# Moving z, the attention matrix and the transposes of q and v inside a hybrid layer's mixer

## The chip, the cores and the metric

The kernel runs on one core of a Trainium2 chip. The metric is the device time of one execution in microseconds, as the median of three runs. The engines are TensorE (PE, with its weight loads as PEld), VectorE (DVE), ScalarE (ACT), GpSimd (POOL) and SyncE (SP, which issues most DMAs). Each engine works through its own queue of instructions in order; an instruction that waits holds back all that stand behind it on that engine.

## The reference

One layer over 512 positions of width 1024. A mixer with two head groups (a gated delta rule and a sliding-window attention) is followed by a mixture of 32 experts, of which each token uses two.

```python
h = modulate(rms_norm(x, norm_mix[l]), shift1, scale1)
proj = h @ w_in[l]
(g_q, g_k, g_v, g_z, g_a, g_b, s_q, s_k, s_v) = jnp.split(proj, split_points, axis=-1)
gdn_out = gated_deltanet(g_q, g_k, g_v, g_z, g_a, g_b, conv_w[l], a_log[l],
                         dt_bias[l], gdn_out_norm[l])
swa_out = sliding_window_attention(s_q, s_k, s_v, q_norm[l], k_norm[l], sinks[l], positions)
mixed = jnp.concatenate([gdn_out, swa_out], axis=-1) @ w_out[l]
x = x + gate1[:, None, :] * mixed
h2 = modulate(rms_norm(x, norm_ffn[l]), shift2, scale2)
x = x + gate2[:, None, :] * hierarchical_moe(h2, ...)
```

In gated_deltanet q, k and v pass a short convolution with silu; per chunk of 64 positions a unit lower triangular matrix is inverted, `attn = (q k^T) * decay` is formed, and the chunks are scanned with a state. The result is normed and multiplied by silu(z). The sliding-window attention norms q and k, turns them by the angles of their positions (rope), and adds a sink per head to the softmax.

## The kernel before

Every product of the mixer is made in three passes: both operands are split into a high and a low part, and high x high, high x low and low x high are summed (`passes`, lines L263 to L265). A weight is split by ScalarE (high part, L269) and GpSimd (low part, L270) one step ahead of the projection that uses it (`split_w`, called from `project`). A projection of one block of 128 columns of q, k, v or z is 24 products of 128x512 into one bank (p_proj); one of 256 columns of the attention's q, k and v is 96 products of 128x256 (p_nat).

The program writes the mixer as five streams: `delta_rule` (convolution of k, decay, inversion, joins, chunks, gated output), `products` (all projections, the angles, rope's turns and the attention), `ropes`, `modulations` and `out_gdn` (gate rows, output weights, output projection of the delta rule's half). Each stream yields keys, and `weave` always runs the stream with the lowest key next; so the numbers after `yield` set the order in which the instructions are written, and that order is the order of each engine's queue, apart from small shifts by the scheduler.

The names that the change touches:

- `q_block` (L599), `v_block` (L621): after a projection's products the convolution on VectorE (L397, L400), then `to_rows`, four transposes on TensorE (p_q, p_v, L406). Before, these stand in the middle of the next projection's products.
- `attn(n)` (L605): for 128 positions, p_qk on TensorE (L611), the product with the decay on VectorE (an, L614), transposes on TensorE (p_at, L617), a copy on ScalarE (L618). Before, all four run while the blocks are inverted.
- the inversion: 31 steps of two VectorE instructions (prod L643, R L645), then eight transposes on VectorE (tw L657, Mn L662) with copies on ScalarE (TT L659). `join32` (p_y, p_z) and `join64` (p_yy) assemble the blocks on TensorE, and `chunk` scans them.
- `gate_z` (L783): evacuation and silu of one block of z.
- `angles` (L796): p_pos, a transpose of the positions on TensorE, then VectorE (L805 to L815), then a long row of 128x128 instructions on GpSimd (L816 to L834).
- `rope`, `rope_turn`, `attend`: scores p_s, softmax, transposes p_pT, p_av. `gdn_out(n)`: p_ot (L771) and the gated output.
- `gate_rows` (p_gate on TensorE, L986, copy kg on ScalarE, L989), `load_wo` (the output weights scaled by kg on VectorE, L1002, then split: woH on ScalarE, woL on GpSimd for the first four blocks), `router_operands` (p_cst, L1036). `out_half(1, tb, cc)` is 12 products of p_wo for 128 positions and 512 columns and an addition to xr (L1019); eight of these make the delta rule's half, and eight the attention's half follow. Then come routing, the gather of the tokens, and the experts.

Of the kernel before, what the change touches and what calls it, by code (L numbers as in the profile page):

```python
# [13 lines left out]
AF = mybir.ActivationFunctionType  # L14
ALU = mybir.AluOpType
# [4 lines left out]
P = 128  # L20
# [49 lines left out]
def hybrid_layer(ctx, tc, x, c, positions, w_ada, b_ada, norm_mix, w_in, conv_w, a_log, dt_bias,  # L70
# [187 lines left out]
    hH = [hHL[0][kb // 4][:, kb % 4] for kb in range(KB)]  # L258
    hL = [hHL[1][kb // 4][:, kb % 4] for kb in range(KB)]

    def passes(ps, aH, aL, bH, bL, first, last):

        T.matmul(ps, aH, bH, start=first, stop=False)  # L263
        T.matmul(ps, aH, bL, start=False, stop=False)  # L264
        T.matmul(ps, aL, bH, start=False, stop=last)  # L265

    def split(hi, lo, src, eng):

# [130 lines left out]
        A.activation(raw, y, AF.Tanh)  # L399
        V.scalar_tensor_tensor(y, raw, 1.0, y, op0=ALU.add, op1=ALU.mult)  # L400

    def to_rows(src, name):

        pt = pst([P, NT, P], name)
        for tb in range(NT):
            T.transpose(pt[:, tb], src[:, tb * P:(tb + 1) * P], ident)  # L406
        return pt

    def heads(t):
        return t.rearrange("p t (h d) -> p t h d", d=HD)  # L410
# [146 lines left out]
    def split_w(c0, h):  # L557
# [9 lines left out]
            slots.done(f"w{base}")  # L567
        pieces[c0, h] = t

    def project(c0, each, ahead=0):  # L570

        nat = c0 >= C_S
        ps = [psa([P, 2, 256], f"p_nat{c0}_{i}") for i in range(2)] if nat else psa([P, S], f"p_proj{c0 // P}")
        for h in range(2 if nat else 1):
            i = steps.index((c0, h))
            if i + 1 < len(steps):
                split_w(*steps[i + 1])
            w = pieces[c0, h]
            if nat:
                for tb in range(NT):  # L580
                    t = slice(tb * P, (tb + 1) * P)
                    for i in range(4):
                        kb = 4 * h + i

                        passes(ps[tb // 2][:, tb % 2], hH[kb][:, t], hL[kb][:, t], w[:, 0, i], w[:, 1, i],
                               kb == 0 and tb % 2 == 0, kb == KB - 1 and tb % 2 == 1)
            else:
                for kb in range(KB):
                    passes(ps, w[:, 0, kb], w[:, 1, kb], hH[kb], hL[kb], kb == 0, kb == KB - 1)
            slots.done(f"wH{c0}{h}")  # L590
        if nat:
            for tb in range(NT):
                each(tb, ps[tb // 2][:, tb % 2])
        else:
            each(c0 // P, ps)
        load_w(ahead)


    def q_block(cb, ps):  # L599
        qT = big["qT"]  # L600
        raw = big["qraw"][:, cb]
        conv_block(ps, cb, raw, qT[:, cb])
        head_sums(to_rows(qT[:, cb], f"p_q{cb}"), ssq[:, :, 2 * cb:2 * cb + 2], raw)

    def attn(n):  # L605

# [14 lines left out]
    def v_block(cb, ps):  # L621
        b = cb - 8
        t = fill_tile(f"cv{cb}")
        conv_block(ps, cb, big["vraw"][:, b], t)
        v_ = big["vb"][:, :, b * P:(b + 1) * P]
        A.activation(v_, to_rows(t, f"p_v{cb}"), AF.Copy)
        G.tensor_tensor(out=heads(v_), in0=heads(v_), in1=bc2(beta[:, :, 2 * b:2 * b + 2]), op=ALU.mult)


    def invert_prepare():  # L630
# [408 lines left out]


    mod = {}
    GDN_OUT = 112.

    def delta_rule():
        yield 0
# [39 lines left out]
                    hold_slot(f"TT{j}", [P, 16, P])  # L1085
                    G.memset(big[f"TT{j}"], 0.0)
        for cb in range(4):
            yield 66
            invert_finish(cb)
        slots.done("R")  # L1090
        join32(0)
        join64(0)
        join32(1)
        for n in range(NT):
            yield 67
            chunk(n)
            if n + 1 < NT:
                join64(n + 1)
            if n + 2 < NT:
                join32(n + 2)  # L1100
        yield 85
        slots.done("qT", "knat", "knT", "E0", "E1", "TT0", "TT1")
        yield GDN_OUT
        mix_tiles(1)
        for n in range(NT):
            yield GDN_OUT + .1 + 9. * n
            gdn_out(n)
        slots.done("vb", "gz")

    def products():  # L1110
        yield 9
        hold_slot("qT", [P, 4, S])
        hold_slot("qraw", [P, 4, S])
        split_w(*steps[0])
        for i in range(4):
            project(order[i], q_block, 1 - i % 2)
            yield 9 + 5 * i
        slots.done("qraw")
        hold_slot("vb", [P, NT, 512])
        hold_slot("vraw", [P, 4, S])  # L1120
        for i in range(4):
            project(order[4 + i], v_block, i % 2)
            yield 30 + 5 * i
# [5 lines left out]
        slots.done("vraw")  # L1129
        hold_slot("sr", [P, 2, D])  # L1130
        big["skv"] = big["sr"][:, 0].rearrange("p (t n) -> p t n", t=NT)
        project(C_S + 512, keep(big["skv"], 0), 1)
        hold_slot("sq_n", [P, NT, 512])
        yield 57
        project(C_S, keep(big["sq_n"], 0), 1)
        yield 67
        project(C_S + 256, keep(big["sq_n"], 256))
        angles()
# [12 lines left out]
        V.tensor_scalar(nsink, sink, -1.0, None, op0=ALU.mult)  # L1151
        hold_slot("kg", [P, 2, D])
        big["krT"], big["g1"] = big["kg"][:, 0].rearrange("p (k t) -> p k t", t=S), big["kg"][:, 1]
        hold_slot("qrT", [P, 4, S])
        mix_tiles(0)
        for tb in range(NT):
            yield 92.5
            rope_turn(tb)
        for tb in range(NT):
            yield 99. + 12. * tb  # L1160
            attend(tb, 0)
            yield 99. + 12. * tb + 12. / 2
            attend(tb, 1)
        slots.done("qrT", "sq_n", "sr")

    def ropes():
        yield 87.9
        big["ssh"], big["rsh"] = sm("ssh", (P, NT, NR)), sm("rsh", (P, NT, NR))
        for tb in range(NT):
            head_scale(tb)  # L1170
        rsqrt_n(big["rsh"], big["ssh"], 1.0 / HD)
        for tb in range(NT):
            yield 92.2 + 0. * tb
            rope(tb)

    def modulations():
# [14 lines left out]
                columns_e(ada_raw[2], 2, "A2e", 0, 1, col_e[:, 2])  # L1191

    def out_gdn():
        yield 96.
        router_operands()
        gate_rows(big["g1"], mod["g1"])
        xr[0] = pair.tile([P, NT, D], F32, tag="pair", name="xr")
        for i in range(2):
            nc.sync.dma_start(xr[0][:, 2 * i:2 * i + 2], x_view[:, 2 * i:2 * i + 2])
        yield 140.  # L1200
        load_wo(0)
        load_wo(1)
        for tb in range(NT):
            yield max(GDN_OUT + .15 + 9. * tb + 20., 140.)
# [686 lines left out]
```

## Time and profile before

| what | value |
|---|---|
| median of 3 runs | 691.93 us (690.79 to 701.05) |
| the profiled execution | 690.03 us, span 688.0 us |
| mean granted TensorE clock | 0.963 |
| busy in the span: TensorE, VectorE, ScalarE, GpSimd | 90%, 56%, 35%, 26% |
| the chain that ended last | TensorE 45%, DMA 27%, VectorE 20% |

The span is what the profiler saw of the program; the time of the execution has 2.0 us around it. Busy shares are means over stages with different limits, so the rows below are taken by stage.

### The profile page before, as it was taken

What the parts mean: (1) busy time and instruction counts of PE and PEld (TensorE: products, weight loads), DVE (VectorE), ACT (ScalarE), POOL (GpSimd) and SP (SyncE); (2) the same over time, 40 slices, a digit from 0 to 9 for tenths busy, and PEclk for the clock granted to TensorE, in tenths of its full rate; (3) what the DMA queues carried; (4) which work ended last, traced back from release to release, by engine and by line L of the source; (5) the groups of instructions that cost most, each with busy time, mean ns of one, the idle gap of its engine ahead of it and who ended that gap; (6) DMA issues with size and microseconds to landing.
All of it is one profiled execution on the core that took longest, in us unless ns stands there. A gap on an engine that the chain in (4) does not pass through costs nothing.

```text
span 688.0 us, 10766 instructions
## 1 busy us (share of the span) xinstructions
PE 621.2 (90%) x3907; PEld 378.7 (55%) x3908; DVE 387.2 (56%) x808; ACT 243.7 (35%) x546; POOL 182.2 (26%) x259
## 2 busy tenths in 40 slices
PE   6899799988888999988879998899999999999984
PEld 2576554646567978875447887334343334444521
DVE  3343986698999325688887348311342434444724
ACT  3235554232334442328772243413213232222200
POOL 2501315162263386063452002101001121111100
PEclk9799999997999999999989999999999999999998
DMA  8992374174310300251028849599999999999973
GB/s 256 293 318 65 122 279 164 62 250 162 123 61 23 102 2 12 90 216 62 1 64 302 335 156 354 203 399 416 412 414 403 411 410 406 408 408 410 408 296 123
DMA packets 62805, 161.78 MB, mean 235 GB/s; under 512 B 7175, under 2 KB 32931, under 8 KB 56608
## 3 DMA queue, kind: packets, MB, share of 16 engines
q1 hardware_dynamic: 57216, 148.52, 58.3%
q0 software_dynamic: 3952, 6.81, 2.9%
q10 hardware_dynamic: 1584, 5.77, 2.1%
q8 instruction: 31, 0.51, 0.3%
q14 instruction: 22, 0.18, 0.1%
HBM read 158.72 MB, written 8.39 MB: 243 GB/s over the span
## 4 chain that ended last, share of the span: by engine, by line
PE 45%; DMA 27%; DVE 20%; POOL 3%; issue 2%; ACT 2%; SPq 1%; POOLq 0%; ACTq 0%; DVEq 0%
DMA w_p<-in_w_up_dram 15%; DMA w_p<-in_w_down_dram 6%; PE p_gu L1600 5%; PE p_y L1636 3%; DMA w_p<-in_w_gate_dram 3%; DVE prod L643 3%; PE p_proj L265 3%; PE p_proj L263 3%; PE p_proj L264 3%; PE p_wo L264 2%; PE p_wo L265 2%; PE p_wo L263 2%; DVE cv L397 2%; DVE R L645 2%; PE p_ada L284 1%
## 5 line engine op out<-in xcount | busy, mean ns | idle before, releaser
L1600 PE MATMUL p_gu<-w_p,xT 128*32 128x512 f32 (+2 forms) x560 | 95.9, 594 | 0.0
L270 POOL TENSOR_TENSOR wH<-w,wH 128x512 fp32r<-128x512 f32 x36 | 52.4, 1472 | 125.9 <-ACT wH L269 112.8
L1600 PEld LDWEIGHTS p_gu<-w_p,xT 128*32 128x32 f32 (+2 forms) x560 | 32.0, 123 | 61.4 <-issue 55.8
L1519 POOL DMA_INDIRECT gb<-xn_d,ids x16 | 16.2, 1014 | 160.4 <-PE p_x L1587 146.4
L1636 PE MATMUL p_y<-w_p,hT 128*32 128x512 f32 (+2 forms) x280 | 51.3, 597 | 3.7 <-DVE hT L1624 2.6
L1609 DVE TENSOR_TENSOR hid<-hid,p_gu 128x256 f32<-128x256 f32 x16 | 6.7, 421 | 82.6 <-ACT hid L1608 82.6
L1608 ACT ACTIVATE hid<-p_gu 128x256 f32<-128x256 f32 x16 | 6.1, 384 | 126.8 <-PE p_gu L1600 126.8
L1593 ACT ACTIVATE xT<-p_x,sh2e,A2e 128x128 f32<-128x128 f32 x128 | 46.3, 467 | 12.1 <-PE p_x L1587 11.3
L1638 DVE SCALAR_TENSOR_TENSOR y<-p_y,wts,rsl 128x512 f32<-128x512 f32 x32 | 24.0, 749 | 41.5 <-PE p_y L1636 41.5
L265 PE MATMUL p_proj<-hH,wH 128*128 128x512 f32 x96 | 40.8, 425 | 0.0
L263 PE MATMUL p_proj<-hH,wH 128*128 128x512 f32 x96 | 40.5, 422 | 0.0
L264 PE MATMUL p_proj<-hL,wH 128*128 128x512 f32 x96 | 40.0, 417 | 0.0
L1656 PE MATMUL p_add<-yHL,to 128*128 128x512 f32 x128 | 35.5, 417 | 2.9 <-DVE xr L1661 1.9
L1656 PEld LDWEIGHTS p_add<-yHL,to 128*128 128x128 f32 x128 | 21.5, 188 | 19.7 <-DVE xr L1661 8.0
L1636 PEld LDWEIGHTS p_y<-w_p,hT 128*32 128x32 f32 (+2 forms) x280 | 14.8, 122 | 31.0 <-issue 24.4
L1661 DVE TENSOR_TENSOR xr<-xr,p_add 128x512 f32<-128x512 f32 x40 | 26.8, 686 | 6.9 <-PE p_add L1656 6.9
L263 PE MATMUL p_nat<-wH,hH 128*128 128x256 f32 x96 | 28.0, 291 | 0.0
L643 DVE TENSOR_TENSOR prod<-R 128x1 f32<-128x1 f32 (+30 forms) x31 | 27.2, 877 | 0.7
L265 PE MATMUL p_nat<-wH,hL 128*128 128x256 f32 x96 | 27.5, 286 | 0.0
L264 PE MATMUL p_nat<-wH,hH 128*128 128x256 f32 x96 | 27.5, 286 | 0.0
L263 PE MATMUL p_wo<-woH,mH 128*128 128x512 f32 x64 | 25.9, 404 | 0.0
L264 PE MATMUL p_wo<-woL,mH 128*128 128x512 f32 x64 | 25.7, 402 | 0.0
(523 smaller groups left out, 1362.2 us busy)
## 6 DMA issues: line engine op xcount, KB each, us to landing
w_p<-in_w_gate_dram SPq DMA_DIRECT2D x52, 512.0 KB
w_p<-in_w_up_dram SPq DMA_DIRECT2D x52, 512.0 KB
w_p<-in_w_down_dram SPq DMA_DIRECT2D x26, 1024.0 KB
ada<-in_w_ada_dram SPq DMA_DIRECT2D x16, 1024.0 KB
w<-in_w_in_dram SPq DMA_DIRECT2D x9, 1024.0 KB
ada<-in_w_ada_dram SPq DMA_DIRECT2D x12, 512.0 KB
w<-in_w_gate_dram SPq DMA_DIRECT2D x12, 512.0 KB
w<-in_w_up_dram SPq DMA_DIRECT2D x12, 512.0 KB
```

The costliest lines, as they stand in the source:

```text
L263: T.matmul(ps, aH, bH, start=first, stop=False)
L264: T.matmul(ps, aH, bL, start=False, stop=False)
L265: T.matmul(ps, aL, bH, start=False, stop=last)
L270: eng.tensor_tensor(out=lo, in0=src, in1=hi.bitcast(F32), op=ALU.subtract)
L643: V.tensor_tensor(out=pp, in0=Ti[:, :i, :i].rearrange("p j k -> p k j"), in1=Ms[:, :i, i][:, None, :].to_broadcast([P, i, i]), op=ALU.mult)
L1519: nc.gpsimd.indirect_dma_start(out=buf, out_offset=None, in_=xn_d[:, :], in_offset=bass.IndirectOffsetOnAxis(ap=ap, axis=0), bounds_check= ...
L1593: A.activation(self.xT[:, kb], pt[:, i], AF.Identity, bias=sh2e[:, kb:kb + 1], scale=A2e[:, kb:kb + 1])
L1600: self.last = T.matmul(self.ph[r], self.xT[:, kb, r], w[1 + kb // 4][:, :, kb % 4], start=(kb == 0), stop=(kb == KB - 1), tile_position=(0 ...
L1636: self.last = T.matmul(py[o:o + n], self.hT[:, i, o:o + n], w[3][:, i, cs], start=(i == 0), stop=(i == 1), tile_position=(0, o))
L1638: self.made = V.scalar_tensor_tensor(y[:, cs], py, self.w_ap, g2[:, cs], op0=ALU.mult, op1=ALU.mult).ins.name
L1656: t = T.matmul(ps, g_.to[:, tb * P:(tb + 1) * P], g_.yHL[:, i, cs], start=(2 * j + i == 0), stop=(2 * j + i == n - 1))
L1661: return V.tensor_tensor(out=x1(tb)[:, cs], in0=x1(tb)[:, cs], in1=ps, op=ALU.add).ins.name
```

## The change

Products of a projection are remembered by `last_mm`, and the transposes p_q and p_v are ordered behind the last product of the next projection (`rest`, `later`). `attn` moves from the inversion to the places between join and chunk. The keys of the streams change: z is written ahead of the joins, rope and attention are interleaved with the chunks and the gated output (GDN_STEP, ATT), and the gate rows and the output weights come behind the mixer.

```diff
     def passes(ps, aH, aL, bH, bL, first, last):
...
-        T.matmul(ps, aL, bH, start=False, stop=last)
+        last_mm[0] = T.matmul(ps, aL, bH, start=False, stop=last).ins.name
...
-    def to_rows(src, name):
+    def to_rows(src, name, after=None):
 
         pt = pst([P, NT, P], name)
         for tb in range(NT):
-            T.transpose(pt[:, tb], src[:, tb * P:(tb + 1) * P], ident)
+            t = T.transpose(pt[:, tb], src[:, tb * P:(tb + 1) * P], ident)
+            if after:
+                later(t, after)
         return pt
...
             slots.done(f"wH{c0}{h}")
+        while rest:
+            rest.pop(0)(last_mm[0])
         if nat:
...
-        head_sums(to_rows(qT[:, cb], f"p_q{cb}"), ssq[:, :, 2 * cb:2 * cb + 2], raw)
+        rest.append(lambda after: head_sums(to_rows(qT[:, cb], f"p_q{cb}", after), ssq[:, :, 2 * cb:2 * cb + 2], raw))
...
         conv_block(ps, cb, big["vraw"][:, b], t)
-        v_ = big["vb"][:, :, b * P:(b + 1) * P]
-        A.activation(v_, to_rows(t, f"p_v{cb}"), AF.Copy)
-        G.tensor_tensor(out=heads(v_), in0=heads(v_), in1=bc2(beta[:, :, 2 * b:2 * b + 2]), op=ALU.mult)
+
+        def rows_(after):
+            v_ = big["vb"][:, :, b * P:(b + 1) * P]
+            A.activation(v_, to_rows(t, f"p_v{cb}", after), AF.Copy)
+            G.tensor_tensor(out=heads(v_), in0=heads(v_), in1=bc2(beta[:, :, 2 * b:2 * b + 2]), op=ALU.mult)
+        rest.append(rows_)
...
-    GDN_OUT = 112.
+    GDN_OUT, GDN_STEP, ATT = 85., 2.2, 2.2
...
         join32(0)
         join64(0)
+        attn(0)
         join32(1)
         for n in range(NT):
-            yield 67
+            yield 72. + 4 * n
             chunk(n)
             if n + 1 < NT:
+                attn(n + 1)
                 join64(n + 1)
...
-                for n in range(NT):
-                    attn(n)
...
-        yield 78
         project(C_Z, gate_z, 1)
-        yield 82
+        yield 64
         project(C_Z + P, gate_z)
-        yield 88
+        yield 67
         project(C_Z + 2 * P, gate_z)
-        yield 92
+        yield 70
         project(C_Z + 3 * P, gate_z)
...
         for tb in range(NT):
-            yield 99. + 12. * tb
+            yield 75.3 + ATT * 2 * tb
             attend(tb, 0)
...
     def out_gdn():
-        yield 96.
+        yield 92.5
         router_operands()
         gate_rows(big["g1"], mod["g1"])
...
-        yield 140.
+        yield 92.6
         load_wo(0)
         load_wo(1)
```

In the queues this looks as follows (the changed kernel's lines have numbers that are 2 to 12 higher). On GpSimd before, around the angles, the low splits of z's third block (wH17920) stand among the angles' last instructions and those of the fourth (wH19200) behind them:

```order
L794 TENSOR_TENSOR ang_1984<-ang_1984 128x128
L826 TENSOR_SCALAR sin_w_1999<-sin_w_1999 128x128
L793 TENSOR_SCALAR ang_1984<-ang_1984 128x128
L270 TENSOR_TENSOR wH17920_2531<-w1792_2528,wH17920_2531 128x512
L794 TENSOR_TENSOR ang_1984<-ang_1984,sin_w_1999 128x128
L270 TENSOR_TENSOR wH17920_2531<-w1792_2528,wH17920_2531 128x512
L828 TENSOR_TENSOR sin_w_1999<-ang_1984 128x128
L834 TENSOR_TENSOR sr_1584<-ang_1984,qkn_616 128x128
L829 TENSOR_SCALAR ang_1984<-sin_w_1999 128x128
L834 TENSOR_TENSOR sr_1584<-ang_1984,qkn_616 128x128 x7
L270 TENSOR_TENSOR wH19200_2604<-w1792_2528,wH19200_2604 128x512 x2
```

On GpSimd now, at the same place, both stand behind the angles' last instruction (the splits of the first two blocks, wH15360 and wH16640, stand ahead of the angles in both kernels):

```order
L805 TENSOR_TENSOR ang_1872<-ang_1872,sin_w_1887 128x128
L839 TENSOR_TENSOR sin_w_1887<-ang_1872 128x128
L845 TENSOR_TENSOR sr_1473<-ang_1872,qkn_616 128x128
L840 TENSOR_SCALAR ang_1872<-sin_w_1887 128x128
L845 TENSOR_TENSOR sr_1473<-ang_1872,qkn_616 128x128 x7
L272 TENSOR_TENSOR wH17920_1968<-w1792_1961,wH17920_1968 128x512 x2
L272 TENSOR_TENSOR wH19200_2006<-w1792_1961,wH19200_2006 128x512 x2
```

On TensorE before, the first join (p_y0, p_z0) begins right behind p_pos, and the products of z's first block (p_proj12) are woven into it:

```order
L803 MATMUL p_pos_1987<-ident_125,posf_1985 128x4
L673 MATMUL p_y0_2064<-TT0_1730,Mn_1052 32x32 x16
L263 MATMUL p_proj12_2494<-hH0_176,wH15360_1927 128x512
L264 MATMUL p_proj12_2494<-hL0_178,wH15360_1927 128x512
L265 MATMUL p_proj12_2494<-hH0_176,wH15360_1927 128x512
L263 MATMUL p_proj12_2494<-hH0_176,wH15360_1927 128x512
L681 MATMUL p_z0_2084<-y0_2065,Mn_1052 32x32
```

On TensorE now, p_y0 begins behind the last product of z's fourth block (p_proj15); p_pos and 96 products of z stand ahead of it, and the attention's masks (p_s) follow:

```order
L265 MATMUL p_proj15_2043<-hH1_177,wH19200_2006 128x512
L266 MATMUL p_proj15_2043<-hL1_179,wH19200_2006 128x512
L267 MATMUL p_proj15_2043<-hH1_177,wH19200_2006 128x512
L684 MATMUL p_y0_2095<-TT0_1626,Mn_1045 32x32 x16
L905 LDWEIGHTS identb_576
L905 MATMUL p_s000_2659<-maskw_625,identb_576 128x256
```

On TensorE before, at the end of the gated output, p_wo follows the last p_ot at once; p_gate stands some 70 rows earlier, between rope's turns (p_qrT, p_krT) and the first scores:

```order
L921 MATMUL p_pT211_3111<-ident_125,p21_3091 128x128 x4
L929 MATMUL p_av21_3118<-pT210_3109,sr_1584 64x256 x2
L929 MATMUL p_av21_3118<-pT211_3116,sr_1584 64x256 x2
L771 MATMUL p_ot3_3202<-ident_125,vb_1195 128x128 x4
L263 MATMUL p_wo100_3231<-woH0_3213,mH1_2941 128x512
L264 MATMUL p_wo100_3231<-woL0_3214,mH1_2941 128x512
```

On TensorE now, at the same place, the attention's last p_av stands ahead of the last p_ot, and p_cst and p_gate stand between it and p_wo, of which two accumulators are opened with the first woH:

```order
L932 MATMUL p_pT310_3188<-ident_125,p31_3175 128x128 x2
L932 MATMUL p_pT311_3195<-ident_125,p31_3175 128x128 x2
L940 MATMUL p_av31_3202<-pT310_3193,sr_1473 64x256 x2
L940 MATMUL p_av31_3202<-pT311_3200,sr_1473 64x256 x2
L782 MATMUL p_ot3_3219<-ident_125,vb_1188 128x128 x4
L1047 MATMUL p_cst_3234<-rsl_3228,sh2_1253 128x36 x8
L997 MATMUL p_gate_3244<-ident_125,g1_1250 128x128 x4
L997 MATMUL p_gate_3250<-ident_125,g1_1250 128x128 x4
L265 MATMUL p_wo100_3279<-woH0_3261,mH1_3006 128x512
L265 MATMUL p_wo101_3293<-woH0_3261,mH1_3006 128x512
```

## Rows read from the trace of the kernel before

**Rows 1.** Windows by stage: from:to, length, PE, PEld, DVE, ACT, POOL, PEclk, DMA, GB/s.
```profile
144.00:226.60 82.60, 67.88 (x434) 52.26 (x433) 77.54 (x108) 26.08 (x48) 33.13 (x21) 0.88 0.31 110
226.60:238.40 11.80, 11.80 (x108) 11.65 (x107) 0.62 (x3) 5.60 (x14) 5.08 (x4) 1.00 0.29 90
238.40:294.40 56.00, 54.62 (x713) 46.10 (x710) 28.50 (x61) 19.77 (x42) 28.15 (x48) 1.00 0.14 47
294.40:354.40 60.00, 49.65 (x261) 31.36 (x260) 51.11 (x122) 38.01 (x114) 32.79 (x42) 0.91 0.23 84
383.50:418.00 34.50, 33.72 (x194) 27.55 (x193) 16.41 (x51) 13.08 (x24) 4.05 (x6) 1.00 0.70 254
440.00:665.00 225.00, 215.89 (x1198) 90.77 (x1194) 87.73 (x152) 61.31 (x158) 28.95 (x29) 1.00 1.02 407
```

**Rows 2.** Waits of PE, 130 to 245: waited for, us, times, longest.
```profile
PE p_v L406 <- DVE cv L400: 6.2, 2, 3.4
PE p_v L406 <- DVE R L645: 3.2, 1, 3.2
PE p_qk L611 <- DVE an L614: 2.7, 1, 2.7
PE p_col L959 <- ACT modr L952: 2.6, 1, 2.6
```

**Rows 3.** Groups by line, 144 to 227: busy, mean ns, idle before.
```profile
L611 PE MATMUL p_qk<-knT,qT 64*128 64x128 f32 x64 | 8.2, 339 | 2.7 <-DVE an L614 2.7
L617 PE MATMUL p_at<-ident,an 128*128 128x128 f32 x32 | 6.4, 336 | 0.0
L614 DVE TENSOR_TENSOR an<-p_qk,E 128x512 f32<-128x512 f32 x8 | 5.1, 685 | 2.8 <-PE p_qk L611 2.8
```

**Rows 4.** Timeline, the last two tw transposes and ScalarE's copies: start, us.
```profile
220.37 2.05 DVE L657 STREAM_TRANSPOSE tw<-R 32x1024 f32<-32x1024 f32 x1
224.54 2.05 DVE L657 STREAM_TRANSPOSE tw<-R 32x1024 f32<-32x1024 f32 x1
222.46 1.15 ACT L659 ACTIVATE TT<-tw 32x512 f32<-32x512 f32 x2 [3.58 <-DVE tw L657]
```

**Rows 5.** Timeline from p_pos to GpSimd's angles, then the window of the angles.
```profile
238.09 0.22 PE L803 MATMUL p_pos<-ident,posf 4*128 4x4 f32 x1
239.45 2.60 POOL L270 TENSOR_TENSOR wH<-w,wH 128x512 fp32r<-128x512 f32 x2 [3.84 <-ACT wH L269]
243.20 0.40 POOL L816 TENSOR_TENSOR sin_w<-ang 128x128 f32<-128x128 f32 x1 [1.14 <-DVE ang L815]
...
243.20:262.80 19.60, 18.90 (x300) 16.10 (x301) 4.94 (x10) 8.87 (x19) 18.87 (x39) 1.00 0.01 3
```

**Rows 6.** Window behind the wait of p_qk.
```profile
160.00:170.00 10.00, 10.00 (x47) 7.45 (x48) 7.52 (x14) 2.62 (x5) 1.05 (x1) 0.54 0.19 79
```

**Rows 7.** Gate rows and output weights: timeline, then groups from 240 to 430.
```profile
314.36 2.05 PE L986 MATMUL p_gate<-ident,g 128*128 128x128 f32 x16 [0.47 <-ACT qrT L873]
316.45 0.60 ACT L989 ACTIVATE kg<-p_gate 128x512 f32<-128x512 f32 x1
317.08 1.22 DVE L1002 TENSOR_TENSOR wo<-wo,kg 128x1024 f32<-128x1024 f32 x1 [1.93 <-ACT kg L989]
319.83 1.06 ACT L269 ACTIVATE woH<-wo 128x1024 fp32r<-128x1024 f32 x1
320.97 2.35 POOL L270 TENSOR_TENSOR woL<-wo,woH 128x1024 fp32r<-128x1024 f32 x1 [0.48 <-ACT woH L269]
353.72 2.87 POOL L270 TENSOR_TENSOR woL<-wo,woH 128x1024 fp32r<-128x1024 f32 x1
...
L270 POOL TENSOR_TENSOR woL<-wo,woH 128x1024 fp32r<-128x1024 f32 x4 | 10.2, 2545 | 3.4 <-ACT woH L269 3.3
L1036 PE MATMUL p_cst<-rsl,sh 128*128 128x36 f32 x16 | 1.9, 273 | 0.0
```

**Rows 8.** Timeline, the last p_ot, first p_wo, the first half's last addition.
```profile
354.39 0.66 PE L771 MATMUL p_ot<-ident,vb 128*128 128x128 f32 x4 [1.53 <-DVE vb L768]
354.80 0.48 PE L263 MATMUL p_wo<-woH,mH 128*128 128x512 f32 x1
355.12 0.39 PE L264 MATMUL p_wo<-woL,mH 128*128 128x512 f32 x1
355.35 0.39 PE L265 MATMUL p_wo<-woH,mL 128*128 128x512 f32 x1
383.32 0.69 DVE L1019 TENSOR_TENSOR xr<-xr,p_wo 128x512 f32<-128x512 f32 x1 [2.03 <-PE p_wo L265]
```

More of the change, by code (lines that the diff above doesn't have):

```diff
@@ L259, in hybrid_layer @@
     hL = [hHL[1][kb // 4][:, kb % 4] for kb in range(KB)]
+    last_mm = [None]
     def passes(ps, aH, aL, bH, bL, first, last):
@@ L568, in split_w @@
         pieces[c0, h] = t
+    rest = []
     def project(c0, each, ahead=0):
@@ L1087, in delta_rule @@
         for cb in range(4):
-            yield 66
+            yield 70.6
             invert_finish(cb)
@@ L1100, in delta_rule @@
                 join32(n + 2)
-        yield 85
+        yield 84.5
         slots.done("qT", "knat", "knT", "E0", "E1", "TT0", "TT1")
-        yield GDN_OUT
         mix_tiles(1)
         for n in range(NT):
-            yield GDN_OUT + .1 + 9. * n
+            yield GDN_OUT + GDN_STEP * n
             gdn_out(n)
@@ L1117, in products @@
             yield 9 + 5 * i
-        slots.done("qraw")
         hold_slot("vb", [P, NT, 512])
@@ L1122, in products @@
             project(order[4 + i], v_block, i % 2)
+            if i == 0:
+                slots.done("qraw")
             yield 30 + 5 * i
@@ L1126, in products @@
                 G.tensor_tensor(out=rq2, in0=rq, in1=rq, op=ALU.mult)
-                for n in range(NT):
-                    attn(n)
-        slots.done("vraw")
         hold_slot("sr", [P, 2, D])
@@ L1132, in products @@
         project(C_S + 512, keep(big["skv"], 0), 1)
+        slots.done("vraw")
         hold_slot("sq_n", [P, NT, 512])
-        yield 57
+        yield 50
         project(C_S, keep(big["sq_n"], 0), 1)
-        yield 67
+        yield 56
         project(C_S + 256, keep(big["sq_n"], 256))
+        yield 61
         angles()
         hold_slot("gz", [P, 4, S])
-        yield 78
         project(C_Z, gate_z, 1)
-        yield 82
+        yield 64
         project(C_Z + P, gate_z)
-        yield 88
+        yield 67
         project(C_Z + 2 * P, gate_z)
-        yield 92
+        yield 70
         project(C_Z + 3 * P, gate_z)
@@ L1151, in products @@
         V.tensor_scalar(nsink, sink, -1.0, None, op0=ALU.mult)
+        yield 70.9
         hold_slot("kg", [P, 2, D])
@@ L1156, in products @@
         for tb in range(NT):
-            yield 92.5
+            yield 73.2 + 2. * tb
             rope_turn(tb)
         for tb in range(NT):
-            yield 99. + 12. * tb
+            yield 75.3 + ATT * 2 * tb
             attend(tb, 0)
-            yield 99. + 12. * tb + 12. / 2
+            yield 75.3 + ATT * (2 * tb + 1)
             attend(tb, 1)
@@ L1166, in ropes @@
     def ropes():
-        yield 87.9
+        yield 71.
         big["ssh"], big["rsh"] = sm("ssh", (P, NT, NR)), sm("rsh", (P, NT, NR))
@@ L1172, in ropes @@
         for tb in range(NT):
-            yield 92.2 + 0. * tb
+            yield 73.1 + 2. * tb
             rope(tb)
@@ L1203, in out_gdn @@
         for tb in range(NT):
-            yield max(GDN_OUT + .15 + 9. * tb + 20., 140.)
+            yield 93. + .1 * tb
             for cc in range(2):
```

## The prediction

> **What bounds the kernel now.** I read the page first, then the table of stages, then the waits of TensorE, then single instructions where the change moves them. The stages [rows 1] show one chain with a different limit in each part. From 144.0 to 226.6 us VectorE is the limit: it is busy 77.54 of 82.60 us with the triangular inversion, while TensorE is busy 67.88. From 226.6 to 238.4 TensorE is the limit (11.80 of 11.80): the inversion is done and the last projections are still being multiplied. From 238.4 to 294.4, the joins and chunks, TensorE is busy 54.62 of 56.00 us and VectorE only 28.50. From 294.4 to 354.4, rope and attention, it is the other way: VectorE 51.11 of 60.00, TensorE 49.65 and its clock at .91. After 440 the experts' weights come in at a DMA share of 1.02. The experts' stream follows the routing, and the routing follows the output projection, so a shift of the mixer's end is taken over by the end of the program as it stands. That is the quantity to forecast: when the first half of the output projection ends, now at about 383.3 us, where the last of its eight sums is added [rows 8].
>
> **Stalls that go.** In the inversion's stretch TensorE waits for VectorE at p_v (6.2 + 3.2 us) and p_qk (2.7), and for ScalarE at p_col (2.6) [rows 2]. The transposes p_v now stand behind the next projection's 24 products, which gives cv a projection's time to be ready, so the first two go; p_qk leaves the stretch with `attn`. VectorE gains what matters more: the eight `an` products are 5.1 us, and the idle time ahead of them, for p_qk, is 2.8 [rows 3]. That is 7.9 us, and the last transpose of the inversion, which now ends at 224.54 + 2.05 = 226.6 [rows 4], comes at 226.6 - 7.9 = 218.7.
>
> **The z projections.** All 96 products now stand on TensorE ahead of join32(0). They need weights split by ScalarE (high part) and GpSimd (low part), one step ahead. GpSimd's own queue is the point: the splits of z0 and z1 stand before the angles, those of z2 and z3 behind all of them. Before, z2's splits stood in the middle of the angles and TensorE had joins to do meanwhile; now it has nothing behind z1 until z2's weights come.
>
> The time of that, step by step. The high split of the last projection's second half stands on ScalarE behind the copies of the third transpose tw. Before, that transpose ends at 220.37 + 2.05 = 222.4 and its copies take 1.15 [rows 4]; now 7.9 earlier, 214.5 and 215.7. An evacuation (1.2) and the split (1.16) follow: 218. The low part takes 2.60 for two [rows 5], so 220.6, and half of a 96-product projection behind it, 48 products at 11.80 / 108 = .11 us each [rows 1], is 5.3: p_pos comes at 224 to 226, against 238.09. From p_pos to GpSimd's first angle takes 243.20 - 238.09 = 5.1 us [rows 5], with 2.5 as the least, since the VectorE angles in it are some 2.6 without the gaps: 226.5 to 231. GpSimd works through the angles from 243.2 to 262.8, with hardly a gap (18.87 us busy) [rows 5]; two single splits lie in it, 1.3 each by the 2.60 for two, so the angles alone take 17: their end is at 243.5 to 248. The low split of z2 starts there, 1.3 for its first half, and the 24 products at .23 each, the pitch from 355.12 to 355.35 [rows 8], take 5.5; z3's weights are split meanwhile, and it takes 5.5 more. Join32(0) so begins at 256 to 260.5 without any loss of clock, in place of 238.4.
>
> TensorE waits here for some 10 us. What that does to the clock has rows for short waits only: behind the p_qk wait of 2.7 us the granted clock was .54 for 160 to 170 us [rows 6], near the lower level of 1.2 GHz, and the work of those 10 us then took its full length. I take 2 us, between 0 (no fall) and 5.5 (all of z2 at half speed), nearer to the fall, since this wait is much longer than 2.7. The Trainium skill, "TensorE: Matmul & The Clock Gate", section "What's actually happening", says that the clock drops to half after an idle stretch and returns after sustained work. By that rule the fall is certain here; the sum would keep its 2 us, and without the rule it could drop to 0.
>
> So the joins start at 258 to 262.5 with the 2 us: I take 260, which is **21.6 us later** than before. The low end is 248, if ScalarE's split and the angles' gaps both fall best and GpSimd runs its angles faster beside an idle VectorE; the high end is 264.
>
> **From the joins to the last attention.** Before, this took 354.4 - 238.4 = 116.0 us, in which TensorE was busy 54.62 + 49.65 = 104.3 and idle 11.7. The z products go (96 x .23 = 21.8), and p_cst and p_gate (1.9 + 2.05 [rows 7]) move behind it. The products of `attn` come in: p_qk 8.2 and p_at 6.4 us of busy time [rows 3], which overlap in the pipeline; issue to issue I count 8.9 for both. TensorE's sum is 104.3 - 21.8 - 4.0 + 8.9 = 87.4. VectorE's is 28.50 + 51.11 = 79.6, plus `an` 5.1, minus the angles and the scaling of wo that lie elsewhere now, near 77. Both are close to each other, so neither hides wholly behind the other in queues that run in order. With the idle time of before, 87.4 + 11.7 = **99 us**. Its bounds are 88, if rope and attention fill every gap between the chunks, and 106, at the busy share that TensorE has from 294.4 to 354.4 (87.4 / (49.65 / 60.00)). With 260 + 99 the last p_ot comes at 359, against 354.4. Of the 21.6 us 17 are so given back.
>
> **The tail.** Before, the factors of the output weights lay beside the attention: p_gate at 314.36, the first woL at 320.97, the fourth at 353.72, one before the first p_wo product at 354.80 [rows 7, 8]. Now p_cst and p_gate stand on TensorE behind the last p_ot, and everything hangs on them in a row: p_cst 1.9, p_gate 2.05, the copy kg .60, the scaling on VectorE 1.22, woH 1.06, woL 2.55 [rows 7]: 9.4 us until the first woL is ready, at 368.4. Three more follow on GpSimd at 2.55 each: 376. Two of the eight accumulators are opened meanwhile, so that at 376 or 377 two of eight are done, and six remain at 12 products x .23 = 2.72: 377 + 16.3 = 393.5. Against 383.3 this is **10 us later**. The gap of before between p_ot and p_wo was none, so the serial chain is a new wait; that the attention no longer shares TensorE with p_wo (the last p_av came at 366 before) pays for half of it.
>
> The half that follows (from 383.5 to 418.0, TensorE 33.72 of 34.50 busy [rows 1]) is bound by its own products and goes with the shift.
>
> **The sum.** +21.6 (joins) - 17 (116.0 to 99) gives +4.6 at the last p_ot, and the tail makes it +10.4. The profiled execution of before took 690.03 us for a span of 688.0; 690.03 + 10.4 = 700.4. The median of the runs shown is 691.93, 1.9 above the profiled one; on it the forecast is 691.93 + 10.4 = **702 us**, 1.5% slower. The measurement of this kernel can tell about 2%, 13.8 us, from no change.
>
> **Rivals.**
> Faster: the wait for z2 is short and the overlap works. Joins at 248, the stretch at TensorE's sum of 88, so the last p_ot at 336, and the tail of 34.5 us behind it: 370.5, which is 12.8 earlier than 383.3, or 679 us. For it speaks that VectorE is idle for half of the joins now (28.50 of 56.00); against it the order of GpSimd's queue. Past 2% only if both go best: .09.
>
> Slower: the angles hold the joins until 263 and the stretch takes 106, because in TensorE's single queue each chunk's product that waits for VectorE or ScalarE also holds back the attention's products behind it. Last p_ot at 369, end of the half at 403.5: +20, 712 us. It passes 2% from a stretch of 102.5 with the joins at 260. For it speaks the .91 clock and the 10 us idle of 294.4 to 354.4; against it that the chunks' stretch had only 1.4 us idle. A chance of .33, with worse cases to 718.
>
> No change: the moved parts only trade places, and the tail's serial chain is covered because ScalarE and GpSimd are quiet there (woL at 2.35 rather than 2.55, the first accumulators done while the later woL are split). The last p_ot at 352 and the end of the half at 385: within 4 us, 688 to 696. A chance of .18.
>
> **How the numbers follow.** The forecast of +5 to +14 has .40, no change .18, slower .33, faster .09. Faster by over 2%: .09; slower by over 2%: .34; the rest, .57, within. The range of 684 to 717 takes in the joins from 250 to 263 and the stretch from 90 to 106; it leaves out most of the fast case and the worst of the slow one.
>
> **What would show it.** In the profile after: tw's last transpose ends near 219; TensorE has a wait of some 10 us on GpSimd's split ahead of z2; the first p_y near 260; the last p_ot near 359; between it and steady p_wo products a wait on woL of GpSimd; the half's last sum near 393. I am wrong if the z2 wait is missing or if the stretch from the first p_y to the last p_ot is under 92 us or over 106.

## The result and the profile after

The changed kernel takes 744.03 us (739.78 to 754.39, 4 runs) against 691.36 before: a ratio of 1.077, 95% interval 1.067 to 1.088. The forecast was 702 with 717 as the upper end. Most kernels here had faster and slower executions: the medians are of all of them, the ratios of the faster ones against those of the kernel before that ran beside them, and the first profile came from a slower one (754.39 us, 14 us late already where the inversion begins), so the lines below are from a second profile of the same kernel, an execution of 744.17 us.

First the stages, with the columns of [rows 1]: to the last tw transpose's start, from there to the first p_y, to the last p_ot, to the last addition of p_wo.

```profile
144.00:216.40 72.40, 54.90 (x372) 44.40 (x370) 70.93 (x95) 22.03 (x46) 38.07 (x22) 0.93 0.33 111
216.40:263.30 46.90, 33.16 (x145) 27.91 (x145) 8.50 (x14) 11.13 (x22) 29.25 (x46) 0.78 0.14 45
263.30:393.20 129.90, 114.52 (x973) 87.30 (x976) 70.71 (x183) 56.90 (x160) 27.52 (x43) 0.76 0.13 43
393.20:466.10 72.90, 64.48 (x304) 51.38 (x302) 41.85 (x61) 22.53 (x32) 20.93 (x34) 0.88 0.57 210
```

The inversion is shorter by what was expected, and the joins begin at 263.3. But from there to the last p_ot it takes 129.9 us, where 99 were forecast, and TensorE is busy 114.5 of them at a granted clock of 0.76. The attention's last p_av is in there too (391.0). The same four points in the timeline:

```profile
216.43 1.95 DVE L668 STREAM_TRANSPOSE tw<-R 32x1024 f32<-32x1024 f32 x1
226.71 0.22 PE L814 MATMUL p_pos<-ident,posf 4*128 4x4 f32 x1
263.31 0.69 PE L684 MATMUL p_y<-TT,Mn 32*32 32x32 f32 x32
392.82 0.66 PE L782 MATMUL p_ot<-ident,vb 128*128 128x128 f32 x4 [1.45 <-DVE vb L779]
435.49 0.69 DVE L1030 TENSOR_TENSOR xr<-xr,p_wo 128x512 f32<-128x512 f32 x1 [2.03 <-PE p_wo L267]
```

They answer to [rows 4], [rows 5] and [rows 8]: 226.6 has become 218.4, 238.1 is 226.7, and the last addition of the first half has gone from 383.32 to 435.49. TensorE's waits from 200 to 420 us (columns of [rows 2]):

```profile
PE p_proj L267 <- POOL wH L272: 12.2, 1, 12.2
PE p_wo L266 <- POOL woL L272: 5.4, 4, 2.2
PE p_zz L710 <- ACT yy L707: 5.1, 3, 3.5
PE p_nat L265 <- ACT wH L271: 4.9, 1, 4.9
PE p_wo L265 <- ACT woH L271: 3.0, 1, 3.0
```

The 12.2 is the wait for z2's weights behind the angles. The other new waits are short. What is long is the work itself; the joins and the first chunk in windows of 8 us (last columns: granted clock, DMA share, GB/s):

```profile
264.00:272.00 8.00, 6.13 (x94) 5.21 (x95) 2.25 (x4) 2.98 (x8) 2.43 (x4) 0.79 0.18 22
272.00:280.00 8.00, 7.45 (x105) 6.17 (x103) 4.22 (x7) 4.07 (x9) 0.00 (x0) 0.50 0.01 2
280.00:288.00 8.00, 7.31 (x35) 7.12 (x34) 4.15 (x17) 0.85 (x2) 0.96 (x2) 0.50 0.01 2
288.00:296.00 8.00, 7.55 (x43) 6.17 (x42) 4.79 (x11) 1.83 (x4) 4.43 (x11) 0.50 0.00 0
296.00:304.00 8.00, 7.20 (x109) 6.23 (x110) 4.24 (x9) 3.15 (x8) 1.73 (x5) 0.50 0.01 2
```

From 272 to 304 us TensorE is busy for more than nine tenths of the time, and its clock is at the lower level, 1.2 GHz, throughout. It falls in the window ahead of that, in which TensorE waits for ScalarE, 0.92 us at p_yy and 0.68 at p_zz. Before, the joins and chunks had 1.00 throughout [rows 1].

### The profile page after: what moved, and what is told of

It reads as the page before. It is cut to its first block, busy times and chain, and to the rows that moved or that the text cites. A ratio compares the mean times of both kernels' runs of the same rounds, so it can differ in the third digit from the quotient of the medians.

```text
span 752.7 us, 10754 instructions
## 1 busy us (share of the span) xinstructions
PE 658.3 (87%) x3903; PEld 408.4 (54%) x3908; DVE 387.3 (51%) x808; ACT 246.3 (33%) x546; POOL 188.1 (25%) x259
## 4 chain that ended last, share of the span: by engine, by line
PE 60%; DVE 19%; DMA 7%; POOL 7%; issue 2%; ACT 2%; SPq 1%; POOLq 0%; ACTq 0%; DVEq 0%
PE p_gu L1612 13%; PE p_y L1648 7%; DVE prod L654 4%; DMA w_p<-in_w_down_dram 4%; PE p_add L1668 3%; PE p_proj L265 2%; PE p_proj L267 2%; PE p_proj L266 2%; DVE R L656 2%; POOL woL L272 2%; PE p_wo L266 2%; PE p_wo L267 2%; PE p_wo L265 2%; DMA w_p<-in_w_up_dram 2%; PE p_ada L958 2%
## 5 line engine op out<-in xcount | busy, mean ns | idle before, releaser
L267 PE MATMUL p_proj<-hH,wH 128*128 128x512 f32 x96 | 40.6, 423 | 12.2 <-POOL wH L272 12.2
L265 PE MATMUL p_nat<-wH,hH 128*128 128x256 f32 x96 | 29.0, 302 | 5.6 <-ACT wH L271 5.6
L654 DVE TENSOR_TENSOR prod<-R 128x1 f32<-128x1 f32 (+30 forms) x31 | 30.7, 989 | 0.7
L266 PE MATMUL p_nat<-wH,hH 128*128 128x256 f32 x96 | 28.4, 296 | 0.8 <-POOL wH L272 0.8
L267 PEld LDWEIGHTS p_proj<-hH,wH 128*128 128x128 f32 x96 | 19.5, 203 | 17.6 <-POOL wH L272 12.6
```

Of the source, the lines that this page charges most:

```text
L267: last_mm[0] = T.matmul(ps, aL, bH, start=False, stop=last).ins.name
L654: V.tensor_tensor(out=pp, in0=Ti[:, :i, :i].rearrange("p j k -> p k j"), in1=Ms[:, :i, i][:, None, :].to_broadcast([P, i, i]), op=ALU.mult)
```

## The experiments

The theories: **C**, the dense 128x512 products of z, woven into the joins, held TensorE's clock up, and without them the small products run at half clock; **W**, the loss is waits between engines in queues that run in order.

**The same kernel again.**

> The changed kernel once more, for a second profile. Theory C (clock): with z out of the joins, TensorE has only small products (32x32 joins, 64-row p_qk, transposes) between the joins and the attention and its granted clock stays near half for long stretches, so the stretch from the first p_y to the last p_ot again takes 120 to 132 us, with a mean granted clock under 0.8 in it. Theory W (waits): the stretch is long because one in-order queue makes the chunks' products wait for VectorE and ScalarE; then the idle time of TensorE in the stretch is over 25 us and its clock is the result. Time by both 738 to 746.

743.88 us. Stretch 129.9 us, clock 0.76, TensorE idle 15.4 of it, less than the 25 that W asked for: against W.

**z back among the joins, in the changed kernel.**

```diff
         hold_slot("gz", [P, 4, S])
+        yield 72.1
         project(C_Z, gate_z, 1)
-        yield 64
+        yield 72.15
...
-        yield 67
+        yield 76.1
...
-        yield 70
+        yield 76.15
```

> The changed kernel, with z's 96 products written behind chunk 0 and chunk 1 and so woven between the joins' and chunks' products again, as before the change; all else as changed. Theory C: the dense 128x512 products hold the clock at 1.0 in the joins, and the time falls by 25 to 40 us, to 703 to 718, although 21.8 us of products come into the stretch. Theory W: only the wait of 12 us for z2's weights goes, and the same waits stay between chunks and attention: 728 to 735.

728.24 us (ratio 1.046, 1.023 to 1.069), 16 below the changed kernel: the lower end of W's range, 10 above C's. The joins begin at 227.1, but the stretch, 148.2 us with z's 21.8 in it, has a clock of 0.84. The timeline near its start shows why, VectorE's an and TensorE's p_at:

```profile
248.21 0.69 DVE L622 TENSOR_TENSOR an<-p_qk,E 128x512 f32<-128x512 f32 x1 [8.21 <-POOL ang L840]
248.96 1.11 PE L625 MATMUL p_at<-ident,an 128*128 128x128 f32 x4 [6.96 <-DVE an L622]
```

`an` takes a buffer from the same ring of three that the angles' two tiles come from, and waits until GpSimd has read the last of them. Around and behind that wait the clock was at .50 until 256 and at .64 from there to 264. So here both theories hold a part: the clock is higher with z back, and the rest of the gain is lost to a wait.

**The angles out of z's way, two ways, in the changed kernel.** First behind all of z:

```diff
-        angles()
         hold_slot("gz", [P, 4, S])
...
         project(C_Z + 3 * P, gate_z)
+        angles()
```

> The changed kernel, with the angles written behind all four z projections, so that no low split of z stands behind them on GpSimd; z stays ahead of the joins. Theory C: only the z2 wait of 12.2 us and the clock behind it are saved, the rest stays at half clock: 727 to 735. Theory Q (GpSimd's queue was the step that cost most): 715 to 725.

745.41 us (1.068, 1.044 to 1.092): nothing gained, outside both forecasts. The joins begin at 248.8, 14.5 earlier, and the last p_ot comes at 389.5, 3.7 earlier: the stretch has grown to 140.7 us, since p_at now waits 7.7 us for an, and an 9.0 for the angles' buffer. Then ahead of the last three projections:

```diff
+        angles()
         project(C_S + 512, keep(big["skv"], 0), 1)
...
-        angles()
         hold_slot("gz", [P, 4, S])
```

> The changed kernel with the angles alone written ahead of the last three projections; z stays ahead of the joins. The wait of 12.2 us for z2's weights goes, and so does that for the angles' buffers, which took its place when only z's splits were put ahead of the angles. If the waits are the cost: 725 to 733. If the joins' stretch, at half clock, is as long wherever it begins and the attention behind it waits for something else: 738 to 745.

739.06 us (1.066, 1.057 to 1.076), in the second range by the median; two of its four executions took 734.5 and 734.7 us, so some of the wait may come back. The profile is of the longest of the four, 753.53 us. In it TensorE comes to the joins (at 270.6) without a wait and at full clock:

```profile
256.00:264.00 8.00, 8.00 (x36) 6.37 (x35) 0.96 (x1) 3.28 (x6) 5.31 (x4) 1.00 0.15 49
264.00:272.00 8.00, 7.88 (x66) 6.04 (x64) 0.92 (x2) 2.42 (x5) 1.32 (x3) 1.00 0.01 2
272.00:280.00 8.00, 6.25 (x89) 5.68 (x90) 2.02 (x4) 2.24 (x5) 1.69 (x3) 0.63 0.20 22
280.00:288.00 8.00, 7.45 (x106) 6.17 (x103) 4.16 (x7) 4.01 (x9) 0.00 (x0) 0.50 0.01 2
288.00:296.00 8.00, 7.31 (x35) 7.13 (x34) 4.14 (x17) 0.91 (x2) 0.90 (x2) 0.50 0.01 2
```

It is at .50 within some 10 us of joins all the same, and the stretch has its 131.0 us. So the wait for z2 was not what brought the clock down, and removing it does not bring it back. The same two short waits stand where it falls, 0.92 us at p_yy and 0.68 at p_zz.

**z ahead of the joins, alone, in the kernel before.**

```diff
-        yield 67
+        yield 60
         project(C_S + 256, keep(big["sq_n"], 256))
+        yield 61
         angles()
         hold_slot("gz", [P, 4, S])
-        yield 78
+        yield 62
         project(C_Z, gate_z, 1)
-        yield 82
+        yield 64
...
```

> The kernel before, with one part of the change: the keys of the last projection and of z are lowered so that all 96 products of z stand ahead of the first join. Theory C: the joins and chunks lose their dense products and run near half clock: 15 to 35 us slower than before, 706 to 726. Theory W (the interleaving of attention and chunks in the change costs, not z): the wait for z2's weights costs some 10 us and the shorter stretch behind gives it back: 688 to 698.

721.77 us (1.037, 1.025 to 1.050), as C said. The stretch from the first p_y to the last p_ot, before and now:

```profile
238.20:354.80 116.60, 104.87 (x977) 78.05 (x978) 80.06 (x182) 58.37 (x157) 61.33 (x89) 0.96 0.19 66
275.80:392.00 116.20, 106.12 (x900) 78.07 (x901) 76.28 (x180) 56.92 (x157) 36.01 (x47) 0.75 0.17 57
```

Before, it was 116.6 us with z's 21.8 us of products in it, at a clock of 0.96. Without them it is as long, at 0.75: taking 21.8 us of work out of TensorE's busiest stretch gave nothing back there. (Eight products each of p_pT and p_av and five of p_wo, which lay behind the last p_ot before, came in.) The joins begin 37.6 us later, of which z itself is 21.8 and the wait for its weights 12.2. The start of the stretch also shows that idle time is not what keeps the clock down:

```profile
272.00:280.00 8.00, 6.11 (x102) 4.47 (x100) 2.69 (x6) 4.02 (x9) 2.98 (x4) 1.00 0.16 22
280.00:288.00 8.00, 6.45 (x117) 5.87 (x118) 6.67 (x21) 1.97 (x5) 2.29 (x3) 0.62 0.04 4
288.00:296.00 8.00, 7.31 (x35) 7.13 (x35) 3.69 (x10) 1.76 (x4) 7.76 (x22) 0.50 0.00 0
296.00:304.00 8.00, 8.00 (x80) 6.92 (x79) 4.22 (x11) 3.12 (x7) 2.39 (x5) 0.50 0.01 2
```

From 296 to 304 us TensorE is busy all the time and stays at .50. Where the clock falls there are waits again (1.92 us at p_yy, 0.68 at p_zz); the kernel before has one of 1.25 us at its first p_yy and keeps 1.00. Whether the waits or the kind of products bring it down, no run separates.

**More work for TensorE.** Four products of the normed input's block behind each of 16 pieces of the joins and chunks of the changed kernel, into a bank that nobody reads (the block is kept in its buffer until then):

```diff
+        def fill(n=4):
+            ps = psa([P, S], "p_fill")
+            for i in range(n):
+                T.matmul(ps, hH[i][:, 0:P], hH[i], start=True, stop=True)
         join32(0)
+        fill()
         join64(0)
+        fill()
...
```

> The changed kernel with 64 products more: four 128x512 products of a block of the normed input, into a bank that nobody reads, behind each join, chunk and attention matrix. They compute nothing of the layer. At full clock they are 64 x .23 = 14.6 us of TensorE's time. Theory C (the clock): they hold the clock up between the joins and the attention, and the time falls in spite of the added work, by 5 to 20 us, to 724 to 739. Theory F (z's products only filled gaps that the joins' chain of steps has anyway): the time stays or rises by up to 15 us, 743 to 758.

741.36 us (1.068, 1.055 to 1.081): 2.5 below the changed kernel by the medians, no difference that can be told, and between C's range and F's. The stretch is the clearer measure:

```profile
265.50:390.90 125.40, 116.95 (x1040) 85.69 (x1040) 71.60 (x182) 56.81 (x160) 24.13 (x39) 0.89 0.14 51
```

With 14.6 us of useless products (64 x .23, an estimate from their pitch at full clock) it is 4.5 us shorter, 125.4 against 129.9, and the clock 0.89 against 0.76. So the rest got some 19 us shorter. Of that 7 us are idle time of TensorE (15.4 to 8.4), gaps that the added products fill, as F had it; the other 12 are busy time (114.5 to 116.95 - 14.6 = 102.4), which goes with the clock. The groups show it: the changed kernel from 268 to 304 us, all at the low clock; its whole stretch, only partly at the low clock; and this kernel (count | busy, mean ns | idle before):

```profile
L735 PE MATMUL p_vn<-vb,TT 128*128 128x64 f32 x16 | 3.7, 424 | 0.0
L752 PE MATMUL p_o<-vn,E 128*128 128x64 f32 x16 | 3.5, 414 | 0.0
```

```profile
L735 PE MATMUL p_vn<-vb,TT 128*128 128x64 f32 x64 | 9.8, 314 | 0.0
L752 PE MATMUL p_o<-vn,E 128*128 128x64 f32 x64 | 9.7, 310 | 0.1
```

```profile
L735 PE MATMUL p_vn<-vb,TT 128*128 128x64 f32 x64 | 8.0, 276 | 0.0
L752 PE MATMUL p_o<-vn,E 128*128 128x64 f32 x64 | 8.0, 273 | 0.0
```

**The attention matrices back in the inversion** (`attn(0)` and `attn(n + 1)` removed from the chunks, the loop put back behind the second v projection).

> The changed kernel with the attention matrices back in the inversion, all else as changed. Theory C: the small products leave the stretch and lengthen the inversion by 8 us; it comes out at 734 to 746. Theory A (it is the attention matrices between the chunks that make the stretch long): 715 to 728.

723.12 us (1.042, 1.029 to 1.055): A's range. The stretch is 108.0 us, 21.9 shorter, for products that I had counted at 8.9:

```profile
270.50:378.50 108.00, 98.01 (x881) 73.13 (x881) 64.56 (x175) 51.87 (x152) 26.64 (x43) 0.76 0.15 51
```

Of the 21.9 us 16.5 are busy time of TensorE and 5.4 idle time, most of it the wait of p_zz for ScalarE (5.1 to 0.7). The clock is 0.76, as without the edit, so it is not a better clock that saves them. That the products cost 16.5 and not 8.9 because they ran at the low clock fits the numbers, but is argued and not shown.

**The output weights early again.**

```diff
     def out_gdn():
-        yield 92.5
+        yield 77.
...
-        yield 92.6
+        yield 84.6
```

> The changed kernel with the gate rows, the router's operands and the output weights written beside the chunks and the attention again, as before the change. The tail from the last p_ot to the last addition of p_wo was 72.9 us against 59.8 before. If the serial chain to woL is the cost: 728 to 735. If ScalarE, VectorE and GpSimd are then too late with the attention's own work: no change, 740 to 748.

726.62 us (1.049, 1.036 to 1.062), just under the first range: the serial chain cost 17 us net. From the last p_ot to the last addition it is now 44.3 us instead of 72.9, but the stretch ahead of it, which takes some of this work in, is 141.5 instead of 129.9. In the changed kernel the chain looks like this in the timeline from the last p_ot on:

```profile
395.15 3.53 PE L997 MATMUL p_gate<-ident,g 128*128 128x128 f32 x16
398.71 0.60 ACT L1000 ACTIVATE kg<-p_gate 128x512 f32<-128x512 f32 x1 [0.88 <-PE p_gate L997]
399.34 16.72 DVE L1013 TENSOR_TENSOR wo<-wo,kg 128x1024 f32<-128x1024 f32 x7 [2.95 <-ACT kg L1000]
401.74 13.23 POOL L272 TENSOR_TENSOR woL<-wo,woH 128x1024 fp32r<-128x1024 f32 x4 [2.28 <-ACT woH L271]
415.03 0.29 PEld L266 LDWEIGHTS p_wo<-woL,mH 128*128 128x128 f32 x1 [1.70 <-POOL woL L272]
```

**The late transposes alone, in the kernel before** (the diff's lines for `to_rows`, `rest`, `q_block` and `v_block`, and the releases of their two buffers that go with them).

> The kernel before, with one part of the change alone: the transposes of q and v behind the next projection's products. The waits of 9.4 us at p_v go. If VectorE alone sets the inversion's end: no change, within 4 us of before. If TensorE's head start counts (the last projection ended 11.8 us behind the inversion): 6 to 11 us faster.

701.52 against 694.72 us beside it, ratio 1.005 (0.999 to 1.012): nothing gained. TensorE still waits 4.0 us at p_v instead of 9.4, and 5.7 at p_at and 7.5 at p_col instead of 2.7 at p_qk and 2.6 at p_col; the wait has moved.

**Three things undone together, and the angles.**

> The changed kernel with three things undone together: z woven behind chunks 0 and 1, the attention matrices back in the inversion, gate rows and output weights written early. One by one these took 16, 21 and 17 us off. If the three costs are separate they add up: 744 - 54 = 690, the time of before, with only the late transposes and the interleaved rope and attention left of the change. If they are one cost seen three times (the clock), 705 to 720.

707.14 us (1.021, 1.015 to 1.027): 37 of the 52 us, not 54, in the range of one cost seen three times. The program stands still for the angles' buffers once more, this time ScalarE at the norm of q ahead of the join's evacuation, and TensorE behind it for 11.5:

```profile
264.50 0.63 ACT L854 ACTIVATE hsq<-sq_n 128x512 f32<-128x512 f32 x1 [12.78 <-POOL ang L840]
265.04 0.75 ACT L687 ACTIVATE y<-p_y 32x256 f32<-32x256 f32 x2
```

> As combo, and the angles written ahead of the last three projections, in the inversion's stretch where GpSimd is idle half of the time. If the angles still hold the joins or rope: 5 to 12 us below combo. If nobody waits for them any more, or the weights' low splits now wait for them: the same as combo, or some us slower.

706.99 us (1.026, 1.017 to 1.036): the same. The wait at the norm of q is gone, but TensorE waits 10.0 us for the last projection's low split, which now stands behind the angles on GpSimd.

**The angles in buffers of their own** (in z's last gate block and a small tile).

```diff
-        t = fill_tile("ang", (P, 4, NT, HH))
+        t = big["gz"][:, 3].rearrange("p (i t d) -> p i t d", i=4, t=NT)
...
-        w, s1_, c1_ = fill_tile("sin_w", (P, 4, NT, HH))[:, 0], sn_, cs_
+        w, s1_, c1_ = mw.tile([P, NT, HH], F32, tag="sin_w", name="sin_w", bufs=1), sn_, cs_
```

> The changed kernel with z woven behind chunks 0 and 1, gate rows and output weights early, and the angles computed in the last block of z's gate tile and a small tile of their own, so that neither the attention matrices nor z's evacuation nor the norm of q wait for the angles' buffers. The attention matrices stay between the chunks. If that move pays once the clock is held up by z and nobody waits for the angles: 680 to 690. If its products lengthen a stretch in which TensorE is the limit by as much as the inversion gets shorter: 691 to 700. If other waits take the place of those for the buffers: 701 to 712.

> As own_attn, with the attention matrices back in the inversion (combo with the angles' buffers apart). Combo stood still for 12.8 us on ScalarE and TensorE behind the norm of q, which waited for the angles' buffer. If that wait and the half clock behind it are all that is left of the loss: 690 to 696. If not: 702 to 708, as combo.

702.01 (1.012, 1.008 to 1.017) and 699.60 us (1.011, 1.001 to 1.021): the first in its worst range, the second between its two. The wait for the buffers was some 7 us of combo's rest; and with z woven the place of the attention matrices makes no difference that can be told. Some 8 us stay. For these and the late transposes the last two runs left rope, attention and output weights as before:

> The kernel before with two parts of the change: the late transposes of q and v, and the attention matrices between the chunks, beside z, which stays woven there; the angles in buffers of their own. Rope, attention, gate rows and output weights stay where they were. The inversion ends some 8 us earlier, and TensorE gets 8.9 us more to do behind it. If the clock holds at 1.0 in the joins: 683 to 690, faster than before. If the joins then start behind a wait for the last projection's weights with the clock low: 692 to 700.

712.95 us (1.027, 1.020 to 1.034), a miss: slower than own_attn. Three stretches of 16 us in its profile are at or near the lower clock, among them the first joins although z is woven there:

```profile
240.00:256.00 16.00, 16.00 (x147) 12.59 (x145) 2.48 (x4) 3.68 (x8) 15.44 (x32) 0.50 0.01 2
320.00:336.00 16.00, 9.02 (x50) 7.00 (x49) 15.51 (x35) 3.95 (x10) 13.64 (x28) 0.56 0.16 62
360.00:376.00 16.00, 16.00 (x49) 7.86 (x46) 9.47 (x26) 8.73 (x28) 7.08 (x5) 0.50 0.06 16
```

So z among the joins does not hold the clock by itself; TensorE waits 1.6 us at p_yy just ahead of the first of the three. Some 7 us of this execution (716.33 us) were lost earlier still: the inversion begins at 148.7 us, against 141.3 in the profile of the next run, and the clock from 104 to 120 us is 0.50 against 0.90, although both have the same late transposes.

> The kernel before with the late transposes and the angles' own buffers, the attention matrices left in the inversion. If the late transposes are worth nothing because p_qk and p_col take over the wait: 689 to 697, as the late transposes alone. If the shared buffers held anything in the kernel before: 683 to 688.

Inconclusive: two executions took 695 and 698 us, four 710 to 718, with granted clocks of .95 and of .91 to .93; the profile is of the one at 698. No version was faster than the kernel before.

## Why the prediction was wrong

Its steps up to the joins were right in mechanism and a few us short. The inversion ends at 218.4 (218.7 forecast), p_pos stands at 226.7 (224 to 226), GpSimd's angles run from 231.8 to 249.4 (226.5 to 231, and to 243.5 to 248), TensorE waits 12.2 us for z2 (some 10), and the joins begin at 263.3 (260). Where the time went, by the last addition of p_wo, which moved from 414.6 to 466.1, by 51.5 us:

- joins' begin: +25.1 (263.3 - 238.2), forecast +21.6;
- joins to the last p_ot: 129.9 against 116.6, +13.3, forecast -17: the step that failed;
- from there to the last addition: 72.9 against 59.8, +13.1, forecast +5.8.

The step that failed is "TensorE's sum is 104.3 - 21.8 - 4.0 + 8.9 = 87.4", and "with the idle time of before, 87.4 + 11.7 = 99 us". The idle time was near right, 15.4. The sum was not: 114.5. I took the durations at the clocks of before (1.00 in the joins) and subtracted z's products as if the rest kept its speed. The prediction did weigh the clock, but only behind the wait for z2, at 2 us. before_z_ahead shows that taking z out leaves the stretch as long as it was, angles_early that the clock falls without the wait for z2 too, and filler that dense products between the small ones bring much of it back. So the clock has a share, shown by filler: 12 us of busy time between clocks of 0.76 and 0.89, of the 27 that the sum was short.

The sum also put a term at nothing: the attention's last products. Before, 16 each of its p_pT and p_av lay behind the last p_ot (2.1 and 2.2 us of busy time). The change brings them ahead of it; p_av in the stretch, before and now:

```profile
L929 PE MATMUL p_av<-pT,sr 128*64 128x256 f32 x40 | 7.0, 451 | 0.4 <-ACT pT L923 0.4
L940 PE MATMUL p_av<-pT,sr 128*64 128x256 f32 x56 | 9.8, 460 | 0.8 <-ACT pT L934 0.7
```

The prediction used their leaving in the tail, but took p_cst and p_gate out of the stretch without putting these 4.3 us in. What is left of the 27 us no run takes apart.

The rule that the prediction quotes from the Trainium skill, "TensorE: Matmul & The Clock Gate", section "What's actually happening", that the clock falls after an idle stretch, agrees with the drop behind z2's wait (.57 from 248 to 256) but does not cover the fall inside the joins, where TensorE counts as busy for 7.2 to 7.6 of each 8 us.

The attention matrices were mis-sized in the same step: 8.9 us by issue at full clock, 21.9 by attn_back, which overlaps with the clock's share. And they give the inversion less than the 7.9 counted for them: with the matrices back (attn_back) its end is only 3.8 us later, and with the late transposes, no matrices moved and the angles' own buffers (own_rows) the last tw already starts at 219.7 instead of 224.5. Each gives about half, so that the end came as forecast was luck: the prediction gave all of it to the matrices.

In the tail the chain p_cst, p_gate, kg, scaling, woH, woL was right, with two terms too small. p_gate took 3.53 us at the low clock instead of 2.05. And woL came every 3.3 us instead of 2.55, since the scaling of the next weights on VectorE stood beside it (below). The fourth woL was ready 21.8 us behind the last p_ot, against 17 forecast, and the half's last addition 42.3 behind it, against 34.5.

The slower rival had the joins right (263) and the right sign for the stretch, but by a wrong reason, waits in TensorE's queue; TensorE's idle time in the stretch grew by 3.7 us only. The sign that the prediction named for its being wrong, a stretch over 106 us, is what came. That the late transposes do not shorten the whole by themselves was not forecast either: I let two waits at p_v go without asking what waits next.

What stays open: the last 8 us between own_combo and the kernel before, and why own_before loses the clock in its first joins where the kernel before keeps it with nearly the same rows. The runs show where the clock falls, not whether the small products or the short waits among them bring it down, nor which mixture of products would hold it.

## What to carry to other kernels

Before dense products are moved away from small ones, look at the granted clock of both stretches: a duration read at the full clock is no duration for the same instruction in other company, and "busy" in the profile does not say that the clock will stay. When a change moves a step, list the tiles that share its buffers as well as its queues; the angles' two tiles of a ring of three held up the attention matrices in some runs and the norm of q in another. And preparation that costs little beside other work (gate rows, output weights) costs its whole chain when it is put in a row behind it: 28.6 us of tail against 11.6 us of stretch in wo_early.

## What the runs showed of the hardware

TensorE ran 32 us at 1.2 GHz while the profile had it busy for over nine tenths of the time, with 32x32, 64-row and 128x64 products among others, and in before_z_ahead 8 us while busy all the time. 64 products of 128x512 strewn in between made that stretch 4.5 us shorter, not longer (125.4 against 129.9).

VectorE and GpSimd slowed each other where both worked on two operands in SBUF. In wo_early the scaling of the output weights took 1.21 us on VectorE and woL 2.35 on GpSimd. Side by side, in the changed kernel, they took up to 3.39 and 3.30 to 3.35, as if each waited out a part of the other. The Trainium skill, "SBUF — State Buffer", section "SBUF: two separate sides", calls the pair of ports that the two share an exclusive lock, which a VectorE instruction with two inputs in SBUF contends for with one of GpSimd that reads SBUF; the trace agrees, with 3.3 to 3.4 for either, not far under the sum of 2.35 and 1.21.
